# Seven-product matrix multiplication for both feed-forward products, with the squared hidden rows staged in DRAM

## The chip, the cores and the metric

The kernel runs on one core of a Trainium2 chip. TensorE (PE) multiplies matrices into PSUM, VectorE (DVE), ScalarE (ACT) and GpSimd (POOL) work on tiles in SBUF or PSUM, and SyncE (SP) issues most of the DMA transfers. The metric is the time of one execution on the device in microseconds, median of three runs.

## The reference

One step of a two-layer decoder trunk over 1024 prompt tokens and 32 sample tokens (8 sequences of 4), 1056 tokens of width 1024. Everything is fp32.

```python
for i in range(DEPTH):                       # DEPTH = 2
    hp = rms_norm(xp, norm_mix[i]); hs = rms_norm(xs, norm_mix[i])
    if i % N_MIXERS == 0:                    # layer 0: spatial-gating MLP in chunks of 128
        ...
    else:                                    # layer 1: indexer, top 256 keys per query, attention
        ...
    xp = xp + op; xs = xs + os_
    xp = xp + sqrelu_mlp(rms_norm(xp, norm_ffn[i]), ffn_w1[i], ffn_w2[i])
    xs = xs + sqrelu_mlp(rms_norm(xs, norm_ffn[i]), ffn_w1[i], ffn_w2[i])
y = rms_norm(x, norm_final)

def sqrelu_mlp(h, w1, w2):                   # w1: 1024 x 4096, w2: 4096 x 1024
    a = jax.nn.relu(h @ w1)
    return (a * a) @ w2
```

The outputs are the normalized rows, the new keys, values and indexer keys, and the chunk rows of layer 0. The sample sequences attend to 1024 cached positions each, fetched by a page table.

## The kernel before

Tokens lie along the free dimension, features along the 128 partitions. The 1056 tokens form three chunks of 384, 384 and 288 (`CH`). Each fp32 operand of a large product is split in a high and a low part: `split` (L201) writes the high part on ScalarE (L203) and the rest on VectorE (L204), or on GpSimd where `lo_w` says so; with a gain it uses L206 and L207. `mm3` (L240) makes one product of three matmuls (L242, L247, L248): high by high, high by low, low by high.

The residual lies in SBUF as `X`. `out_proj` adds the mixer's projection to it (L500), sums the squares (L299, L300) and splits the gain-scaled rows into `H`; the scale of a token, `rbc`, comes from `norm_chunk` and is applied only after the up product, so the matmuls needn't wait for it.

`ffn` runs over 32 tiles of 128 hidden rows. A tile's up product is plain: 8 products `mm3` for each chunk. VectorE applies relu and `rbc` (L526), ScalarE squares into `st` (L539). Two tiles make a block (`FB`). For 15 of the 16 blocks the down product is in the seven-product scheme: both operands are cut in 2 x 2 parts, seven products of sums of the parts replace eight. The left operand is 256 hidden rows by 256 outputs (four pairs of output tiles, `m`), the right one 256 hidden rows by 528 tokens (two halves, `pr`), so a matmul has 264 columns (`SN`). `combine0` and `combine1` make the right sums on GpSimd (L550 to L558) and split them into `A2`; `w2_block` makes the weights' sums on GpSimd (L568 to L571) and splits 1024 columns. `w2_pair` issues the matmuls (L590 to L592); each result is added into `X`: six on VectorE, `u7` copied by ScalarE (L603) and added twice by GpSimd (all L581). The up products of the next block's first tile stand between the pairs. The last block is plain, with `done` behind each output tile and chunk: `done0` writes the rows to DRAM and splits the next layer's input, `done1` prepares the final norm, and `final` transposes and writes the outputs.

In the attention, `sample_keys` transposes the cached keys of two sequences and computes their dots, `sample_mask` spreads the selection, `sample_softmax` works for one key head over all eight sequences, `fetch_values` reads the values into `H`'s memory, and `sample_values` multiplies.

The order of the instructions on each engine is set by a scheduler that simulates the program when it is built; each engine then works in that order, and tiles of a pool with few buffers are reused in turn.

## Time and profile before

| | |
|---|---|
| median of 3 runs | 2442.8 us (2439.52 to 2445.67) |
| the profiled execution | 2439.28 us, span 2436.9 us |
| TensorE busy | 2336.8 us, 96% |
| weight loads | 2246.2 us, 92% |
| VectorE busy | 1692.9 us, 69% |
| GpSimd busy | 1310.4 us, 54% |
| ScalarE busy | 1062.5 us, 44% |
| TensorE's mean granted clock | 0.982 of full speed |
| DMA | 158.38 MB, mean 65 GB/s |

The busy time of an engine is the union of its instructions. Matmuls are pipelined: one of 264 columns shows as 0.28 us though the next starts long before it ends, so their pace is read from start to start. The span leaves out some 2 us around the program.

### The profile page before, as it was taken

The page shows a single profiled execution, that of the slowest core. Times are in us where ns is not written, and L with a number is a line of the kernel's source. Part 1 is how long each engine was busy: PE and PEld are TensorE (multiplying, and loading weights), DVE is VectorE, ACT ScalarE, POOL GpSimd, SP SyncE. Part 2 cuts the span into 40 slices and gives each one's busy share as a digit, 9 for nine tenths or more (in the row PEclk, how much of TensorE's full clock was granted, in tenths as well). Part 3 has the DMA queues.
Part 4 walks back from the last instruction along what each step waited for, and adds up shares of the span by engine and source line. Part 5 has one row for each costly group of instructions (what it writes and reads, how often), then busy time and mean ns, then how long its engine had stood idle before and what let it go on. Part 6 is the DMA issues. An engine that isn't in the chain of part 4 may idle for free.

```text
span 2436.9 us, 42780 instructions
## 1 busy us (share of the span) xinstructions
PE 2336.8 (96%) x15961; PEld 2246.2 (92%) x15961; DVE 1692.9 (69%) x3732; ACT 1062.5 (44%) x2164; POOL 1310.4 (54%) x1695
## 2 busy tenths in 40 slices
PE   8999999999999999989988968999999999999998
PEld 7999999999999999988988747899999999999998
DVE  6151257777777777774998879735677777777775
ACT  6232243333333333355865767734333333333335
POOL 2245446676676676561224435414566766766754
PEclk9999999999999999999999979999999999999999
DMA  6211301111111111141223441040111111111111
GB/s 231 61 46 35 123 27 46 47 48 49 44 48 48 49 52 40 55 131 30 84 70 104 142 173 27 10 158 27 44 48 45 48 49 45 51 46 49 53 44 72
DMA packets 180800, 158.38 MB, mean 65 GB/s; under 512 B 10376, under 2 KB 169712, under 8 KB 179568
## 3 DMA queue, kind: packets, MB, share of 16 engines
...
q0 software_dynamic: 4096, 18.88, 2.3%
...
## 4 chain that ended last, share of the span: by engine, by line
PE 35%; DVE 9%; POOL 4%; issue 4%; ACT 2%; DMA 1%; SPq 0%; another core or an unknown queue 0%; DVEq 0%; POOLq 0%; ACTq 0%
PE ps L242 4%; PE ps L248 4%; PE ps L247 3%; PE px L242 3%; PE px L248 3%; PE px L247 3%; PE ps L590 2%; PE ps L591 1%; PE ps L592 1%; DVE sc L895 1%; POOL st L558 1%; PE pt L1138 1%; PE pt L592 1%; PE pt L591 1%; PE pt L590 1%
## 5 line engine op out<-in xcount | busy, mean ns | idle before, releaser
L581 POOL TENSOR_TENSOR X<-X,scr 128x264 f32<-128x264 f32 x480 | 427.0, 913 | 165.0 <-DVE X L581 119.4
L248 PE MATMUL ps<-h,w 128*128 128x384 f32 (+1 forms) x1344 | 438.3, 326 | 1.6 <-POOL w L204 1.4
L242 PE MATMUL ps<-h,w 128*128 128x384 f32 (+1 forms) x1344 | 437.1, 325 | 0.7 <-DVE scr L909 0.4
L247 PE MATMUL ps<-h,w 128*128 128x384 f32 (+1 forms) x1344 | 435.8, 324 | 0.0
L203 ACT ACTIVATE w<-raw 128x1024 fp32r<-128x1024 f32 (+2 forms) x248 | 250.6, 1012 | 305.6 <-PE px L247 123.3
L204 DVE TENSOR_TENSOR w<-raw,w 128x1024 fp32r<-128x1024 f32 (+1 forms) x211 | 298.4, 1414 | 32.9 <-ACT w L203 32.6
L242 PE MATMUL px<-h,w 128*128 128x384 f32 (+1 forms) x960 | 310.8, 324 | 0.3
L248 PE MATMUL px<-h,w 128*128 128x384 f32 (+1 forms) x960 | 309.8, 323 | 0.0
L247 PE MATMUL px<-h,w 128*128 128x384 f32 (+1 forms) x960 | 309.2, 322 | 0.0
L603 ACT ACTIVATE scr<-ps 128x264 f32<-128x264 f32 x240 | 92.7, 386 | 426.4 <-PE ps L592 380.3
L248 PEld LDWEIGHTS ps<-h,w 128*128 128x128 f32 x1344 | 254.4, 189 | 3.1 <-POOL w L204 1.7
L242 PEld LDWEIGHTS ps<-h,w 128*128 128x128 f32 x1344 | 254.6, 189 | 2.4 <-ACT w L203 1.0
L247 PEld LDWEIGHTS ps<-h,w 128*128 128x128 f32 x1344 | 254.4, 189 | 0.6
L581 DVE TENSOR_TENSOR X<-X,ps 128x264 f32<-128x264 f32 x480 | 197.4, 422 | 64.3 <-PE ps L592 64.3
L581 DVE TENSOR_TENSOR X<-X,px 128x264 f32<-128x264 f32 x480 | 194.2, 422 | 52.2 <-PE px L592 52.2
L581 DVE TENSOR_TENSOR X<-X,pt 128x264 f32<-128x264 f32 x480 | 203.1, 423 | 33.7 <-PE pt L592 29.0
L590 PE MATMUL ps<-A,w 128*128 128x264 f32 x720 | 206.8, 288 | 20.2 <-ACT A L203 20.2
L591 PE MATMUL ps<-A,w 128*128 128x264 f32 x720 | 206.6, 290 | 7.6 <-DVE A L204 7.5
L592 PE MATMUL ps<-A,w 128*128 128x264 f32 x720 | 203.6, 284 | 0.0
L568 POOL TENSOR_TENSOR raw<-raw 128x128 f32<-128x128 f32 x120 | 56.6, 472 | 267.7 <-DMA raw<-in_ffn_w 178.1
L204 DVE TENSOR_TENSOR A<-st,A 128x264 fp32r<-128x264 f32 (+2 forms) x184 | 164.1, 905 | 45.7 <-ACT A L203 45.6
L242 PEld LDWEIGHTS px<-h,w 128*128 128x128 f32 x960 | 180.4, 188 | 1.3 <-DVE X L581 1.2
...
## 6 DMA issues: line engine op xcount, KB each, us to landing
...
raw<-in_ffn_w SPq DMA_DIRECT2D x120, 256.0 KB
...
```

Of the source, the lines that this page charges most:

```text
L203: S.activation(hi, src, AF.Copy)
L204: (lo_w[0] or V).tensor_tensor(lo, src, f(hi), op=ALU.subtract)
L242: PE.matmul(out, lh, rh, start=first, stop=False)
L247: PE.matmul(out, lh, rl, start=False, stop=False)
L248: PE.matmul(out, ll, rh, start=False, stop=last)
L558: G.tensor_tensor(q[:, 1], q[:, 2], q[:, 1], op=ALU.subtract)
L568: G.tensor_tensor(sm[0], a21, a22, op=ALU.add)
L581: eng.tensor_tensor(x, x, src, op=op)
L590: PE.matmul(p, wh, xh, start=first, stop=False, skip_group_check=not first)
L591: PE.matmul(p, wh, xl, start=False, stop=False, skip_group_check=not first)
L592: PE.matmul(p, wl, xh, start=False, stop=True, skip_group_check=not first)
L603: S.activation(u, p, AF.Copy)
```

## The change

Both feed-forward products are in the seven-product scheme. `wino` issues seven products of `nk` times three matmuls of 264 columns. `out_proj` keeps three residual rows at a time, writes them to DRAM (`x_out`) and leaves gain-scaled rows in `XG`, one tile per half of 528 tokens (`TH`). `combos` makes the seven right sides of the up product for a half, each 4 x 264 columns, and splits them into slots of the pools `c8`, `ca`, `cb` and `cc`. `w1_block` makes the weights of 256 hidden rows. The products are summed into a tile `c` of four quarters, then `squares` applies relu and `rbc`, squares, makes four sums of the squares (`t`) and writes all eight tiles to DRAM, `hd`. The down product runs after the up product is complete: `hidden` reads one right side of 512 hidden rows (540 KB) and splits it, `w2_block` makes the weights, `block` adds the products into `XS` and `U`. The sum `u7` is collected in `U` and added to both its quarters in the last 512 rows. The residual is added by a GpSimd DMA that accumulates, in the third of the eight. In the last 512 rows the first two pairs of output tiles are done whole, the other two by halves of the tokens, with `done` behind each.

The sample attention handles four sequences per group: `sample_keys` does one sequence at a time beside the value tiles, `sample_softmax` both key heads of four sequences, and `fetch_values` comes ahead of it. `H` is one tile, or a list of tiles of `c8`.

```diff
-FB = 2
+NB = DF // 512
-SLOT = {(0, 0): 2, (0, 1): 3, (1, 0): 1, (1, 1): 0}
-PRODS = (("v5", 4, 1, True), ("u1", 0, 0, True), ("v3", 7, 2, False), ("u6", 5, 5, False), ("q4", 3, 4, True),
-         ("p2", 2, 3, True), ("u7", 6, 6, False))
+TH = T // 2
+PRODS = (("v5", True), ("u1", True), ("v3", False), ("u6", False), ("q4", True), ("p2", True), ("u7", False))
+HID = {"u1": 0, "p2": 2, "v3": 3, "v5": 4, "u6": 5, "u7": 6, "q4": 7}
...
+    def out_proj(w, gain, pre, x_in, x_out):
...
         def after(p, o, c, sl):
-            V.tensor_tensor(X[:, o, sl], p, X[:, o, sl], op=ALU.add)
-            sumsq(X[:, o, sl], o, c)
+            x = rows[o][:, sl]
+            V.tensor_tensor(x, p, x, op=ALU.add)
+            sumsq(x, o, sl)
+            for pr in range(2):
+                a, b = max(sl.start, pr * TH), min(sl.stop, (pr + 1) * TH)
+                if a < b:
+                    S.activation(XG[pr][:, o, a - pr * TH:b - pr * TH], rows[o][:, a:b], AF.Copy, scale=gain[:, o:o + 1])
+            if c == NC - 1:
+                SP.dma_start(x_out[o // 2][o % 2], rows[o])
...
+    def wino(nk, wt, xt, pr, post):
+        banks = {}
+        for key, first in PRODS:
+            if first:
+                banks[key[0]] = ps({"u": "ps", "v": "px"}.get(key[0], "pt"))
+            p = banks[key[0]][:, :SN]
+            kw = dict(skip_group_check=not first)
+            for k in range(nk):
+                wh, wl, xh, xl = wt(key, 0, k), wt(key, 1, k), xt(key, pr, 0, k), xt(key, pr, 1, k)
+                PE.matmul(p, wh, xh, start=first and k == 0, stop=False, **kw)
+                PE.matmul(p, wh, xl, start=False, stop=False, **kw)
+                PE.matmul(p, wl, xh, start=False, stop=k == nk - 1, **kw)
+            post(key, p)
+            yield
+    def run(*blocks):
+        for _ in PRODS:
+            for g in blocks:
+                next(g)
+    def summed(outs, add=False):
...
+        def post(key, p):
+            if key == "v5":
+                start(p, 3)
+            elif key == "u1":
+                start(p, 0)
+            elif key == "v3":
+                v3.append(p)
+            elif key == "u6":
+                start(p, 1)
+                V.tensor_tensor(outs[1], v3[0], outs[1], op=ALU.add)
+            elif key == "q4":
+                start(p, 2, ALU.subtract)
+            elif key == "p2":
+                V.tensor_tensor(outs[0], p, outs[0], op=ALU.add)
+            else:
+                V.tensor_tensor(outs[2], p, outs[2], op=ALU.add if add else ALU.subtract)
+                V.tensor_tensor(outs[3], p, outs[3], op=ALU.add)
+        return post
...
+    def w1_block(w1, fb, kk):
...
+        w_sums((s1, s2, s4, s3), a11, a21, a12, a22)
+        wt = {}
+        for key, src in (("v5", s1), ("u1", a11), ("v3", s4), ("u6", s2), ("q4", a22), ("p2", a12), ("u7", s3)):
+            wt[key] = wslot([P, 2, 4, P])
+            split(wt[key][:, 0], wt[key][:, 1], src)
+        return lambda key, z, k: wt[key][:, z, k]
+    def w2_block(w2, fb, m):
...
+        wt = {}
+        for keys, src in ((("v5", "u6"), sm[:, 0:2]), (("u1",), r[:, :, 0, 0]), (("v3", "u7"), sm[:, 2:4]),
+                          (("p2",), r[:, :, 1, 0]), (("q4",), r[:, :, 1, 1])):
+            if keys[0] != "q4":
+                t = wslot([P, 2, 2, 2, P])
+            q = 1 if keys[0] == "q4" else 0
+            if len(keys) == 2:
+                split(t[:, 0], t[:, 1], src)
+            else:
+                split(t[:, 0, q], t[:, 1, q], src)
+            for z, key in enumerate(keys):
+                wt[key] = t[:, :, z + q]
+        return lambda key, z, k: wt[key][:, z, k]
+    def ffn(layer, XG, sx, x_in, done):
...
+        def combos(pr, homes):
+            b11, b12, b21, b22 = (XG[pr][:, 4 * i:4 * i + 4, j * SN:(j + 1) * SN] for i in range(2) for j in range(2))
+            t1, t2, t3, t4 = (raw([P, 4, SN]) for _ in range(4))
+            def put(key, src, eng=None):
+                t = HC[pr][key] = homes[key]([P, 2, 4, SN])
+                lo_w[0] = eng
+                split(t[:, 0], t[:, 1], src)
+                lo_w[0] = None
+            V.tensor_tensor(t1, b12, b11, op=ALU.subtract)
+            put("v5", t1)
+            put("u1", b11)
+            V.tensor_tensor(t3, b22, b12, op=ALU.subtract)
+            put("v3", b22, G)
+            V.tensor_tensor(t2, t3, b11, op=ALU.add)
+            put("u6", t2)
+            V.tensor_tensor(t4, t2, b21, op=ALU.subtract)
+            put("q4", t4)
+            if pr:
+                S.activation(t1, b21, AF.Copy)
+                sx[1].close()
+                st, home = slots("cc", 2)
+                sx.append(st)
+                homes["p2"] = homes["u7"] = home
+                b21 = t1
+            put("p2", b21, G)
+            put("u7", t3)
+        def squares(c4, fb, kk, pr):
+            c = c4.rearrange("p (i j) t -> p i (j t)", i=2)
+            rb = rbc[:, None, pr * TH:(pr + 1) * TH].to_broadcast([P, 2, TH])
+            V.scalar_tensor_tensor(c, c, 0.0, rb, op0=ALU.max, op1=ALU.mult)
+            S.activation(c, c, AF.Square)
+            t = fh.tile([P, 4, SN], F32, name="t")
+            G.tensor_tensor(t[:, 0:4:2], c4[:, 1:4:2], c4[:, 0:2], op=ALU.subtract)
+            G.tensor_tensor(t[:, 1], t[:, 2], c4[:, 0], op=ALU.add)
+            G.tensor_tensor(t[:, 3], t[:, 1], c4[:, 2], op=ALU.subtract)
+            for z, x in ((0, c4), (4, t)):
+                SP.dma_start(hd[fb][z:z + 4, :, kk, pr].rearrange("j p t -> p j t"), x)
...
+        wt = w1_block(w1, 0, 0)
+        combos(0, dict(zip(keys, [ca] * 2 + [c8] * 5)))
+        sx[0].close()
...
+        for fb in range(NB):
+            for kk in range(2):
+                if fb or kk:
+                    wt = w1_block(w1, fb, kk)
                 for pr in range(2):
+                    c4 = fh.tile([P, 4, SN], F32, name="c", bufs=3)
+                    run(wino(4, wt, xt1, pr, summed([c4[:, q] for q in range(4)])))
+                    squares(c4, fb, kk, pr)
+                    if fb == kk == pr == 0:
+                        combos(1, dict(zip(keys, [cb] * 2 + [c8] * 3)))
...
+        XS = [fp.tile([P, 2, T], F32, name="x%d" % m) for m in range(4)]
+        U = [fp.tile([P, 2, SN], F32, name="u%d" % m) for m in range(4)]
...
+        def hidden(fb, some):
+            for key in some:
+                s = (nth[0] + 4) % 10
+                nth[0] += 1
+                t = A2[fb, key] = (c8 if s < 8 else ca)([P, 2, 2, 2, SN])
+                r = raw([P, 2, 2, SN])
+                SP.dma_start(r, hd[fb][HID[key]])
+                split(t[:, 0], t[:, 1], r)
...
+            def by_pool(x, p):
+                s = scr(SN)
+                S.activation(s, p, AF.Copy)
+                G.tensor_tensor(x, x, s, op=ALU.add)
...
+            def post(key, p):
+                if key in ("u1", "p2"):
+                    add(c11, p)
+                elif key in ("v3", "u6"):
+                    add(c12, p)
+                elif key == "q4":
+                    add(c21, p, ALU.subtract)
+                elif fb < NB - 1:
+                    by_pool(c22 if key == "v5" else u, p)
+                elif key == "v5":
+                    add(c22, p)
                 else:
+                    add(u, p)
+                    add(c21, u)
+                    add(c22, u)
+            return wino(2, wt, lambda key, pr, z, k: A2[fb, key][:, z, k, pr], pr, post if fb else post0)
+        hidden(0, keys)
+        for fb in range(NB - 1):
+            for z in range(4):
+                m = z if fb else 3 - z
+                wt = w2_block(w2, fb, m)
+                run(*(block(fb, m, pr, wt) for pr in range(2)))
+                if z < 3:
+                    hidden(fb + 1, keys[z:z + 1])
+                if fb == 2:
+                    G.dma_start(out=XS[m], in_=x_in[m].rearrange("o p t -> p o t"), accum_op=ALU.add)
+            hidden(fb + 1, keys[3:])
+        fb = NB - 1
+        for m in range(2):
+            wt = w2_block(w2, fb, m)
+            run(*(block(fb, m, pr, wt) for pr in range(2)))
+            for i in range(2):
+                done(XS, 2 * m + i, slice(0, T), c8)
+        wts = {m: w2_block(w2, fb, m) for m in (2, 3)}
+        for pr in range(2):
+            run(*(block(fb, m, pr, wts[m]) for m in (2, 3)))
+            for o in range(4, NK):
+                done(XS, o, slice(pr * TH, (pr + 1) * TH), c8)
...
+    def done0(X, o, sl, c8):
+        x = X[o // 2][:, o % 2, sl]
+        SP.dma_start(xb[o // 2][o % 2, :, sl], x)
+        sumsq(x, o, sl)
+        if sl.start == 0:
+            H.append(c8([P, 2, T]))
+        hsplit(x, o, sl, G_MIX[1])
         if o == NK - 1:
+            for c in (range(1, NC) if sl.start else range(1)):
+                norm_chunk(c)
...
     for i in range(NT):
         value_tile(i)
-        if 2 <= i < 8:
-            sample_keys(i - 2)
-    probs = []
-    for kv in range(2):
-        probs.append(scores(0, kv))
-        sample_keys(6 + kv)
-    sample_mask()
-    for kv in range(2):
-        sample_softmax(kv)
+        if i:
+            sample_keys(i - 1)
     fetch_values()
     for z in range(2):
+        sample_softmax(z)
+    probs = [scores(0, kv) for kv in range(2)]
+    for z in range(2):
         sample_values(z)
-    H = hidden_state()
+    hst.close()
+    hst, H = hidden_state("hB")
```

VectorE before, at the start of the first feed-forward block: `h` are the split rows of the last chunk, `dg` the diagonals of the norm, `w` weights of the next up tiles, `scr<-px` the relu pass of the first up product.

```order
L272 TENSOR_SCALAR rst_81<-pt_3248 128x3
L207 SCALAR_TENSOR_TENSOR h2_71<-X_2516,gains_78,h2_71 128x288 x2
L500 TENSOR_TENSOR X_2516<-ps_3294,X_2516 128x288
L207 SCALAR_TENSOR_TENSOR h2_71<-X_2516,gains_78,h2_71 128x288
L283 TENSOR_SCALAR dg_3255<-one_72,rst_81 128x128
L283 TENSOR_SCALAR dg_3258<-one_72,rst_81 128x128
L207 SCALAR_TENSOR_TENSOR h2_71<-X_2516,gains_78,h2_71 128x288 x2
L204 TENSOR_TENSOR w_3585<-raw_3578,w_3584 128x1024
L207 SCALAR_TENSOR_TENSOR h2_71<-X_2516,gains_78,h2_71 128x288
L526 SCALAR_TENSOR_TENSOR scr_3389<-px_3364,rbc_80 128x384
```

VectorE in the changed kernel at the same place: `c` are slots of right sides, `raw` their unsplit sums, `xg0` and `xg1` the gain-scaled rows of the two halves; c_3435 is the right side of the product that TensorE does first.

```order
L661 TENSOR_TENSOR raw_3568<-xg1_2535 128x1056
L221 TENSOR_TENSOR c_3446<-raw_3431,c_3446 128x1056
L221 TENSOR_TENSOR c_3450<-raw_3433,c_3450 128x1056
L221 TENSOR_TENSOR c_3456<-raw_3432,c_3456 128x1056
L664 TENSOR_TENSOR raw_3570<-xg1_2535 128x1056
L221 TENSOR_TENSOR c_3435<-raw_3430,c_3435 128x1056
L666 TENSOR_TENSOR raw_3569<-raw_3570,xg1_2535 128x1056
L221 TENSOR_TENSOR c_3438<-xg0_2539,c_3438 128x1056
L289 TENSOR_SCALAR rst_79<-pt_3365 128x2
L289 TENSOR_SCALAR rst_79<-pt_3365 32x1
L668 TENSOR_TENSOR raw_3571<-raw_3569,xg1_2535 128x1056
L221 TENSOR_TENSOR c_3584<-raw_3569,c_3584 128x1056
```

The splits of single tiles' chunks have become splits of 1056 columns, and that of the first product's right side stands fourth among them. On ScalarE its high part comes after the writes of the residual rows to DRAM, since its slot lies on their memory.

VectorE before, at the end of a block of the down product: adds into `X`, weights of 1024 columns, and splits of the next block's right sides into `A2`.

```order
L204 TENSOR_TENSOR A2_3357<-st_6466,A2_3357 128x264
L581 TENSOR_TENSOR X_2516<-X_2516,ps_6602 128x264
L581 TENSOR_TENSOR X_2516<-X_2516,pt_6638 128x264
L526 SCALAR_TENSOR_TENSOR scr_6700<-ps_6675,rbc_80 128x384
L204 TENSOR_TENSOR w_6899<-raw_6892,w_6898 128x1024
L204 TENSOR_TENSOR A2_3357<-scr_6657,A2_3357 128x264
L526 SCALAR_TENSOR_TENSOR scr_6729<-px_6704,rbc_80 128x384
L204 TENSOR_TENSOR A2_3357<-scr_6663,A2_3357 128x264
L526 SCALAR_TENSOR_TENSOR scr_6765<-ps_6740,rbc_80 128x288
L204 TENSOR_TENSOR A2_3357<-st_6355,A2_3357 128x528
L581 TENSOR_TENSOR X_2516<-X_2516,ps_6802 128x264
```

VectorE in the changed kernel between two groups of 512 hidden rows of the down product: adds into `x3`, the last pair's tile, splits of the next group's right sides (`c`), then its first weights (`w`).

```order
L221 TENSOR_TENSOR c_10203<-raw_10204,c_10203 128x1056
L737 TENSOR_TENSOR x3_7331<-x3_7331,px_10084 128x264
L737 TENSOR_TENSOR x3_7331<-x3_7331,px_10094 128x264
L221 TENSOR_TENSOR c_10208<-raw_10209,c_10208 128x1056
L737 TENSOR_TENSOR x3_7331<-x3_7331,ps_10104 128x264
L221 TENSOR_TENSOR c_10213<-raw_10214,c_10213 128x1056
L737 TENSOR_TENSOR x3_7331<-x3_7331,pt_10164 128x264
L221 TENSOR_TENSOR w_10225<-raw_10219,w_10225 128x512
L221 TENSOR_TENSOR w_10228<-raw_10218,w_10228 128x256
L737 TENSOR_TENSOR x3_7331<-x3_7331,ps_10112 128x264
L221 TENSOR_TENSOR w_10231<-raw_10219,w_10231 128x512
L737 TENSOR_TENSOR x3_7331<-x3_7331,pt_10172 128x264
```

Four splits of 1056 columns (the first stands five rows ahead of these) are now among the last pair's adds, where splits of 264 to 792 columns stood, and the next group's weights come behind them.

## Rows read from the trace of the kernel before

**Rows 1.** Busy time in four stretches (us: stretch, length, engines, TensorE's clock, DMA share, GB/s).

```profile
338.70:1067.30 728.60, 712.50 (x4993) 704.66 (x4991) 556.52 (x1090) 276.38 (x571) 470.40 (x610) 1.00 0.17 52
1693.90:2424.20 730.30, 715.96 (x5029) 709.09 (x5027) 545.93 (x1080) 277.71 (x575) 470.49 (x615) 1.00 0.15 46
1067.30:1100.00 32.70, 26.23 (x174) 23.73 (x174) 18.65 (x41) 9.09 (x21) 22.96 (x47) 0.85 0.33 101
2424.20:2437.00 12.80, 5.94 (x55) 5.54 (x53) 4.98 (x9) 5.75 (x12) 3.55 (x5) 0.92 0.69 264
```

**Rows 2.** Timeline of TensorE: first and last matmul of three runs (start us, us, instruction).

```profile
221.33 0.34 PE L242 MATMUL ps<-h,w 128*128 128x384 f32 x1
...
237.91 0.34 PE L248 MATMUL ps<-h,w 128*128 128x384 f32 x1
238.09 0.29 PE L242 MATMUL ps<-h,w 128*128 128x288 f32 x1
...
244.35 0.29 PE L248 MATMUL ps<-h,w 128*128 128x288 f32 x1
...
2378.11 0.29 PE L590 MATMUL ps<-A,w 128*128 128x264 f32 x1
...
2383.09 0.28 PE L592 MATMUL pt<-A,w 128*128 128x264 f32 x1
```

**Rows 3.** TensorE's waits, 338.7 to 1067.3 (us in total, times, longest us).

```profile
PE ps L590 <- ACT A L203: 10.2, 14, 0.8
PE ps L591 <- DVE A L204: 4.2, 13, 0.7
```

**Rows 4.** VectorE by line and form (count; busy us, mean ns; idle before, releasers).

```profile
L204 DVE TENSOR_TENSOR w<-raw,w 128x1024 fp32r<-128x1024 f32 x203 | 290.5, 1431 | 32.9 <-ACT w L203 32.6 <-issue 0.3
L581 DVE TENSOR_TENSOR X<-X,pt 128x264 f32<-128x264 f32 x480 | 203.1, 423 | 33.7 <-PE pt L592 29.0
...
L204 DVE TENSOR_TENSOR A<-st,A 128x528 fp32r<-128x528 f32 x64 | 54.2, 847 | 16.3 <-ACT A L203 16.2
...
L204 DVE TENSOR_TENSOR A<-st,A 128x264 fp32r<-128x264 f32 x60 | 37.7, 628 | 1.6 <-ACT A L203 1.6
L207 DVE SCALAR_TENSOR_TENSOR h<-X,gains,h 128x384 fp32r<-128x384 f32 x48 | 37.5, 804 | 3.8 <-ACT h L206 3.7
L526 DVE SCALAR_TENSOR_TENSOR scr<-ps,rbc 128x384 f32<-128x384 f32 x64 | 35.4, 554 | 118.6 <-PE ps L248 71.4 <-ACT w L203 38.2 <-ACT scr L603 4.7
```

**Rows 5.** ScalarE by line and form.

```profile
L203 ACT ACTIVATE w<-raw 128x1024 fp32r<-128x1024 f32 x220 | 233.1, 1060 | 290.0 <-PE px L247 123.3 <-PE ps L591 72.2 <-POOL raw L571 37.5
L603 ACT ACTIVATE scr<-ps 128x264 f32<-128x264 f32 x240 | 92.7, 386 | 426.4 <-PE ps L592 380.3 <-POOL X L581 46.1
...
L203 ACT ACTIVATE A<-st 128x528 fp32r<-128x528 f32 x64 | 40.9, 640 | 1.0
```

**Rows 6.** Waits of the DMA queue's engine.

```profile
SPq L921 <- DMA qd<-scr: 16.1, 6, 5.2
```

**Rows 7.** Timeline of TensorE at the end of the first feed-forward block.

```profile
1067.13 0.30 PE L248 MATMUL ps<-A,w 128*128 128x288 f32 x1
...
1070.13 0.42 PE L242 MATMUL ps<-w,h 128*32 128x292 f32 x1 [2.15 <-ACT h L206]
1070.35 0.45 PE L247 MATMUL ps<-w,h 128*32 128x292 f32 x1
1070.60 0.45 PE L248 MATMUL ps<-w,h 128*32 128x292 f32 x1
```

**Rows 8.** GpSimd by line and form.

```profile
L581 POOL TENSOR_TENSOR X<-X,scr 128x264 f32<-128x264 f32 x480 | 427.0, 913 | 165.0 <-DVE X L581 119.4 <-ACT scr L603 30.8 <-DVE w L204 12.8
...
L204 POOL TENSOR_TENSOR w<-raw,w 128x512 fp32r<-128x512 f32 x20 | 26.2, 1320 | 77.5 <-ACT w L203 69.5 <-DVE idh L470 7.8
```

**Rows 9.** Timeline of ScalarE in the attention stretch.

```profile
1422.19 0.63 ACT L203 ACTIVATE t<-raw 128x512 fp32r<-128x512 f32 x1 [10.19 <-issue]
```

**Rows 10.** Timeline of VectorE in the same stretch.

```profile
1423.30 0.16 DVE L967 RECIPROCAL rc<-sd 128x1 f32<-128x1 f32 x1 [7.58 <-ACT w L966]
```

425 lines of the change are left out of this document (191 added, 234 removed).

## The prediction

> **What bounds the kernel now.** I read the summary by engine first: TensorE is busy for 96% of the span, VectorE 69%, GpSimd 54%, ScalarE 44%. Then the busy time by stretches: the two feed-forward blocks, from their first up matmul to their last down matmul, last 728.60 and 730.30 us [rows 1], 60% of the span, and TensorE works for 98% of that at its full clock (1.00, the 2.4 GHz level). So I price this change in matmuls first and in waits of TensorE second. The timeline of TensorE gives the pace, start to start: 96 matmuls of 384 columns from 221.33 to 237.91 us, (237.91 − 221.33)/95 = 0.1745 us; 48 of 288 columns, (244.35 − 238.09)/47 = 0.1332; 42 of 264 columns, (2383.09 − 2378.11)/41 = 0.1215 [rows 2]. Last I read TensorE's waits in the first block: the largest two are for the split of the hidden rows, 14 times and 13 times, at most 0.8 us each [rows 3].
>
> By these paces one feed-forward block is 1536 × 0.1745 + 768 × 0.1332 (up product) + 2520 × 0.1215 (15 down blocks) + 96 × 0.1745 + 48 × 0.1332 (the last, plain block) = 268.0 + 102.3 + 306.2 + 16.8 + 6.4 = 699.7 us. The stretches are 28.9 and 30.6 us longer: 59.5 us is lost today, in many gaps of under a microsecond.
>
> **What the matmuls give.** After: up 8 × 2 × 2 × 7 × 4 × 3 = 2688 matmuls, down 8 × 4 × 2 × 7 × 2 × 3 = 2688, all of 264 columns: 5376 × 0.1215 = 653.2 us. That is 46.5 us less per block, **−93.0** for both. This part is firm; the rest is how much more TensorE waits.
>
> **Start of each block.** The first product's right side is now a combination made of the gain-scaled rows. The order shows that its split comes after three other splits, and its slots lie where the residual rows were, so it also waits until these are written to DRAM. From the last matmul of the projection: the add (0.55 us at 384 columns, like the eviction in rows 4), the write of the rows, the high part on ScalarE (1.06, rows 5), before the first matmul. The nearest row of a wait for a DRAM write is 16.1 us in 6 times, mean 2.7, longest 5.2 [rows 6]; I take 3.5 for half a megabyte. The Trainium skill (DMA: Bandwidth & Descriptors, Anatomy of one DMA) gives about 2.0 us fixed plus bytes over 436 GB/s for a transfer; for 540 KB that makes an estimate of 3.2 us, inside this row's span, so the sum by it would be 0.3 us lower at each place. Gap: 0.55 + 3.5 + 1.06 = 5 us. After a gap TensorE comes back at half its clock: at 1070.13, after 2.15 us idle, 292-column matmuls start 0.24 us apart instead of 0.13 [rows 7]; over the 32.7 us around it the mean clock is 0.85, at most 0.15 × 32.7 = 4.9 us lost [rows 1]. I take 3. Price 8 us per block; 0 if the splits run ahead under the projection, 15 if the landing takes the longest row twice.
>
> **Steady up product.** A weight unit is 168 matmuls = 20.4 us of TensorE. VectorE has 7 splits of 128x512 (0.85, by the 128x528 row), 8 adds (0.42) and two passes over 1056 (1.431 × 1056/1024 = 1.475): 6.0 + 3.4 + 3.0 = 12.4 us [rows 4]. GpSimd: 4 sums of 512 (1.32, the row of its 128x512 split) and two sets of three, 2 × (1.35 + 2 × 0.913): 11.6 us [rows 8]. ScalarE: 8 copies at 0.386, 2 squares at 1.1, 7 high parts at about 0.6: 9.5 [rows 5]. All have room; I leave 5 us per block for stray waits.
>
> **Between the products.** Four sum tiles of the down product lie on memory that the square tiles hold until their last write to DRAM has left. From the last up matmul: two adds 0.84, the relu pass 1.475, the square 1.1, GpSimd's three sums 3.2, the write 3.5, the copy into the tile 0.39: 10.5 us. TensorE meanwhile has 8 groups of 6 matmuls, 48 × 0.1215 = 5.8 us, before all its banks are full. Stall 4.7, half clock 3: **8 us** per block (2 to 16).
>
> **Steady down product.** Per 512 hidden rows TensorE has 4 output pairs × 2 halves × 7 × 2 × 3 = 336 matmuls, × 0.1215 = 40.8 us. VectorE: 40 adds × 0.422 = 16.9; weights 4 × (2 × 0.85 + 3 × 0.628) = 14.3; 7 splits of 1056, 7 × 1.475 = 10.3; together 41.5 us [rows 4]. So VectorE becomes the second bound, level with TensorE, and in its row it is not evenly loaded: three pairs have 4.2 + 3.6 + 1.5 = 9.3 us beside 10.2 us of TensorE, but the fourth has four of the splits, 4.2 + 3.6 + 5.9 = 13.7, ahead of the next block's weights. TensorE waits there for 3.5 us, since the banks of the adds queued behind come free late: 6 boundaries × 3.5 = **21 us** per block. Floor 0 (the adds and splits here are means under GpSimd's competition, and slack of the other pairs may absorb the surge), ceiling 46 (VectorE never gets beyond 85% busy: 41.5/0.85 = 48.8, 8 us more per boundary, less the first).
>
> **Last 512 rows.** VectorE takes all sums itself: 72 × 0.422 = 30.4, weights 14.3: 4 us over TensorE's 40.8. In the first block eight splits of the next layer's input come on top: 1056 columns at 0.804/384 per column, 2.2 us, 17.7 in all, of which the last four half-columns fall behind the end anyway. I take +14 and +6 (4 to 22 for the pair's dearer one).
>
> Losses then: first block 8 + 5 + 8 + 21 + 14 = 56, second 8 + 5 + 8 + 21 + 6 = 48; together 104 against today's 59.5: **+44.5**.
>
> **The ends.** The last step now closes 528 tokens at once instead of 288. The end after the last matmul takes 12.80 us now, at 264 GB/s [rows 1]; three more tiles of 0.52 MB at that rate are 6.0 us, with their evictions **+7** (2 to 12). The first block's end, for the same reason, +2.
>
> **Sample attention.** Groups of four sequences put the keys' work beside the value tiles and the value fetch ahead of the softmax. Today ScalarE sits 10.19 us and VectorE 7.58 us idle near 1412 to 1423 us [rows 9, 10]; that may go, at most −12 with what follows it. Against it, value reads of 8 MB now run beside the softmax and delay the prompt's probabilities: +12. I take **0**.
>
> Sum against the profiled execution, 2439.28 us (span 2436.9 and 2.4 around it): −93.0 + 44.5 + 7 + 2 = −39.5, 2399.8. The median of the runs shown is 3.5 above the profiled one, so 2403.
>
> **Rivals.**
> *The waits are hidden.* VectorE's means fall when GpSimd stops adding 480 times into X (rows 8 shows 427 us of it), a boundary costs 1 us and a start 3: losses 3 + 5 + 8 + 6 + 14 = 36 and 28, net −93 + 64 − 59.5 + 9 = −79.5: 2363 (2340 to 2380). For it: today VectorE, at 76% in the block, makes TensorE wait little. Against: the splits now stand four in a row.
> *Dearer joints.* Starts and joints at their upper ends (15 and 16), attention +6: +7 × 2 + 8 × 2 + 6 = 36 above the forecast: 2439, within a few us of no change.
> *VectorE decides: slower.* In the down product VectorE, at 41.5 us of work against 40.8, runs in order with adds that wait for matmuls and splits that wait for ScalarE and for DRAM reads; at 85% a block is 48.8 us, 4.5 more than forecast, × 12 = 54: 2457. It decides from 39.5/12 = 3.3 us above my price, some 47.6 us per 512 rows. For it: nowhere in these stretches is VectorE above 76%. Against: adds released early pair well with long splits.
> *Square tiles hold up the up product: slower.* One buffer takes the sums of squares; its next use waits for its write to land. Each half has 10.2 us; sums 3.2 + write 5.2 + queueing behind half-megabyte weight reads on the same queue could exceed it. At 2 us for each of 64 halves: +128, 2531. Against: 3.2 + 3.5 = 6.7 fits.
> *A matmul has a fixed price, so more matmuls are slower.* The counts go from 4968 to 5376 per block. By rows 2 the price per column is (0.1745 − 0.1215)/120 = 0.44 ns and only 5 ns are fixed, which denies it; if it were all fixed, 699.7/4968 = 0.1408 each, a block's matmuls would take 57 us more, and the kernel 2443 + 115 + 53.5 = 2611. The Trainium skill (TensorE: Matmul & The Clock Gate, Back-to-back issue gap) gives sustained 81 ns at 128 columns and 131 at 512; by that, an estimate of 99, 102 and 114 ns at our widths, a block's matmuls would take 12 us more and the kernel 2443 + 24 + 53.5 = 2520. The trace has 0.1215 us where this says 0.099 and 0.1745 where it says 0.114: the rows decide.
>
> **How the numbers follow.** Forecast 0.45, its own range 2380 to 2430 (floors and ceilings of boundary and joints half used); hidden waits 0.23; dearer joints 0.12; VectorE decides 0.13; square tiles 0.05; fixed price 0.02. About 0.3% (7 us) can be told from no change. Faster: 0.45 + 0.23 and a little of the third, 0.70. The same: most of the third, 0.10. Slower: the last three, 0.20. Range 2355 to 2460: it leaves out the low half of the hidden waits (0.10) and the last two rivals with a tail (0.10).
>
> **What would show it.** Matmuls at 264 columns 0.1215 us apart throughout; blocks of 653 us plus 48 to 56; a gap of 5 us with the half clock at each block's start and between its products; TensorE's longest waits in the down product at the blocks' first pairs, released by VectorE; VectorE above 85% there. The prediction is wrong if the up product waits for GpSimd or DRAM writes in every unit, if blocks of the down product take under 42 us or over 47, or if the attention stretch moves by more than 12 us.

## The result: slower, and the profile after

The changed kernel takes 2497.51 us (median of 4 runs, 2495.17 to 2501.59) against 2442.3 for the kernel before: ratio 1.0234, 95% interval 1.0221 to 1.0247. The forecast was 2403, with a range up to 2460. The span of the profiled execution grew from 2436.9 to 2499.5 us. Its page, first the engines, then TensorE's share and granted clock in 40 slices:

```profile
PE 2299.6 (92%) x16817; PEld 2198.9 (88%) x16817; DVE 1685.8 (67%) x3214; ACT 1204.2 (48%) x2385; POOL 1275.8 (51%) x1287
...
PE   8999879999979899989988989997999997989997
...
PEclk9999989999989999989999979998999998999998
```

TensorE has less to do and waits more; the clock falls at new places. By matmul starts the 62.6 us come from: the first projection ends 10.4 us later (338.94 before, 349.34 now); its gap to the first product grew from 0.13 to 9.7 us, in both layers (+19.1); the two feed-forward blocks, first to last matmul, take 745.8 and 740.0 us instead of 728.1 and 729.6 (+28.1); the stretch between them is 1.0 longer, the end 3.9.

The first block in stretches that follow its work (columns as in [rows 1]): first weight unit, the other fifteen but the last's end, change from up to down product with the first group of 512 hidden rows, groups two to seven, last group.

```profile
359.04:389.90 30.86, 25.31 (x179) 24.80 (x180) 26.92 (x29) 16.90 (x26) 18.65 (x9) 0.80 0.27 82
389.90:697.50 307.60, 306.13 (x2511) 305.91 (x2509) 203.51 (x257) 134.89 (x253) 180.66 (x147) 1.00 0.51 167
697.50:759.50 62.00, 47.61 (x348) 47.19 (x349) 29.20 (x49) 31.75 (x71) 24.59 (x25) 0.86 0.38 123
759.50:805.30 45.80, 42.47 (x338) 41.34 (x336) 38.30 (x67) 21.34 (x45) 29.42 (x30) 1.00 0.43 137
805.30:859.30 54.00, 45.43 (x338) 44.05 (x337) 43.93 (x70) 21.65 (x47) 35.53 (x37) 0.94 0.70 173
859.30:908.30 49.00, 43.53 (x338) 42.75 (x337) 38.81 (x66) 19.65 (x41) 28.99 (x33) 0.97 0.50 141
908.30:955.60 47.30, 43.86 (x339) 42.79 (x337) 38.72 (x71) 21.68 (x47) 31.93 (x32) 0.96 0.41 128
955.60:1002.80 47.20, 42.23 (x336) 41.37 (x337) 39.10 (x69) 20.54 (x44) 33.22 (x34) 1.00 0.41 126
1002.80:1046.00 43.20, 41.77 (x339) 41.13 (x337) 38.32 (x63) 19.15 (x41) 30.77 (x31) 1.00 0.41 125
1046.00:1104.90 58.90, 52.76 (x390) 49.85 (x390) 54.79 (x111) 29.51 (x56) 32.99 (x32) 0.94 0.35 119
```

A weight unit at the pace of [rows 2] is 20.4 us, a group 40.8. The up product's steady part runs at that pace (units of 20.5 us) although VectorE, ScalarE and GpSimd all work there. Nearly everything is lost at joints, where one stage hands over to the next, and in the last group. TensorE's waits from the end of the projection to the end of the block, against the many short ones of [rows 3]:

```profile
PE px L560 <- ACT w L220: 20.0, 14, 3.8
PE px L560 <- ACT x L746: 10.8, 1, 10.8
PE pt L301 <- DVE dg L300: 6.4, 2, 4.7
PE px L561 <- DVE c L221: 5.5, 1, 5.5
```

The largest sum is for the high part of the first weights of a group (L220), not for VectorE's adds. A wait costs more than itself: behind a longer one matmuls start 0.22 us apart instead of 0.1215, which is the lower level of the clock, 1.2 GHz, and the mean granted clock of those stretches is 0.94 to 0.97. In groups two to seven that holds for 61 matmuls of the first block and 80 of the second, 6 and 8 us.

GpSimd's, ScalarE's and TensorE's timelines at the boundary before 908 us show why the weights come late; their load was issued at 892.25 and had landed at 895.8.

```profile
897.75 0.75 POOL L742 TENSOR_TENSOR u<-u,scr 128x264 f32<-128x264 f32 x1 [5.81 <-ACT scr L741]
899.09 1.47 POOL L742 TENSOR_TENSOR u<-u,scr 128x264 f32<-128x264 f32 x1 [0.58 <-ACT scr L741]
900.52 1.48 POOL L742 TENSOR_TENSOR x<-x,scr 128x264 f32<-128x264 f32 x2
901.95 0.74 POOL L602 TENSOR_TENSOR raw<-raw 128x256 f32<-128x256 f32 x1
902.65 1.76 POOL L605 TENSOR_TENSOR raw<-raw 128x256 f32<-128x256 f32 x1
```

```profile
906.14 0.94 ACT L220 ACTIVATE w<-raw 128x512 fp32r<-128x512 f32 x2 [2.21 <-POOL raw L603]
```

```profile
906.82 0.39 PE L560 MATMUL px<-c,w 128*128 128x264 f32 x1 [1.36 <-ACT w L220]
```

GpSimd stands idle for 5.8 us with the weights' sums queued behind additions that wait for ScalarE's copy of a product not yet done. Only then come the sums, the second of them 1.76 us long beside VectorE's splits where the first took 0.74, then ScalarE's high part and the matmul.

### The profile page after: what moved, and what is told of

Same layout as the page of the kernel before. It is cut to its first block, busy times and chain, and to the rows that moved or that the text cites. A ratio compares the mean times of both kernels' runs of the same rounds, so it can differ in the third digit from the quotient of the medians.

```text
span 2499.5 us, 44052 instructions
## 1 busy us (share of the span) xinstructions
PE 2299.6 (92%) x16817; PEld 2198.9 (88%) x16817; DVE 1685.8 (67%) x3214; ACT 1204.2 (48%) x2385; POOL 1275.8 (51%) x1287
## 5 line engine op out<-in xcount | busy, mean ns | idle before, releaser
L221 DVE TENSOR_TENSOR w<-raw,w 128x512 fp32r<-128x512 f32 (+3 forms) x567 | 473.9, 856 | 153.9 <-ACT w L220 145.8
L220 ACT ACTIVATE w<-raw 128x512 fp32r<-128x512 f32 (+3 forms) x604 | 334.6, 582 | 321.0 <-POOL raw L603 155.5
L560 PE MATMUL ps<-c,w 128*128 128x264 f32 x1536 | 442.8, 290 | 11.2 <-DVE x L737 8.2
L561 PE MATMUL ps<-c,w 128*128 128x264 f32 x1536 | 441.0, 288 | 0.0
L562 PE MATMUL ps<-c,w 128*128 128x264 f32 x1536 | 435.3, 287 | 0.0
L560 PE MATMUL px<-c,w 128*128 128x264 f32 x1024 | 298.5, 292 | 59.2 <-ACT w L220 35.3
L560 PE MATMUL pt<-c,w 128*128 128x264 f32 x1024 | 297.9, 291 | 11.5 <-DVE x L737 9.7
L560 PEld LDWEIGHTS ps<-c,w 128*128 128x128 f32 x1536 | 294.7, 192 | 15.2 <-DVE x L737 10.0
L561 PE MATMUL px<-c,w 128*128 128x264 f32 x1024 | 295.4, 289 | 11.1 <-DVE c L221 11.1
L562 PE MATMUL pt<-c,w 128*128 128x264 f32 x1024 | 293.3, 289 | 7.1 <-DVE w L221 7.1
L562 PE MATMUL px<-c,w 128*128 128x264 f32 x1024 | 293.3, 290 | 3.1 <-DVE w L221 3.1
L561 PE MATMUL pt<-c,w 128*128 128x264 f32 x1024 | 295.7, 289 | 0.0
L561 PEld LDWEIGHTS ps<-c,w 128*128 128x128 f32 x1536 | 294.6, 192 | 0.0
L562 PEld LDWEIGHTS ps<-c,w 128*128 128x128 f32 x1536 | 292.0, 192 | 0.0
L560 PEld LDWEIGHTS px<-c,w 128*128 128x128 f32 x1024 | 197.3, 193 | 66.0 <-ACT w L220 40.9
L221 DVE TENSOR_TENSOR c<-raw,c 128x1056 fp32r<-128x1056 f32 x128 | 202.2, 1587 | 36.7 <-ACT c L220 36.1
L560 PEld LDWEIGHTS pt<-c,w 128*128 128x128 f32 x1024 | 196.9, 192 | 14.0 <-DVE x L737 11.4
L561 PEld LDWEIGHTS px<-c,w 128*128 128x128 f32 x1024 | 197.2, 193 | 11.7 <-DVE c L221 11.7
L562 PEld LDWEIGHTS pt<-c,w 128*128 128x128 f32 x1024 | 195.9, 192 | 8.2 <-DVE w L221 8.2
L562 PEld LDWEIGHTS px<-c,w 128*128 128x128 f32 x1024 | 196.7, 194 | 3.9 <-DVE w L221 3.7
L561 PEld LDWEIGHTS pt<-c,w 128*128 128x128 f32 x1024 | 197.2, 193 | 0.0
L602 POOL TENSOR_TENSOR raw<-raw 128x256 f32<-128x256 f32 (+1 forms) x96 | 123.0, 1281 | 144.1 <-DVE c L221 64.0
## 6 DMA issues: line engine op xcount, KB each, us to landing
x<-xa POOLq DMA_DIRECT2D x4, 1056.0 KB, 10.3
```

Of the source, the lines that this page charges most:

```text
L220: S.activation(hi, src, AF.Copy)
L221: (lo_w[0] or V).tensor_tensor(lo, src, f(hi), op=ALU.subtract)
L560: PE.matmul(p, wh, xh, start=first and k == 0, stop=False, **kw)
L561: PE.matmul(p, wh, xl, start=False, stop=False, **kw)
L562: PE.matmul(p, wl, xh, start=False, stop=k == nk - 1, **kw)
L602: G.tensor_tensor(s1, a21, a22, op=ALU.add)
```

## The experiments

All times are medians of 4 to 10 runs beside runs of the kernel before on the same chip (2439 to 2441 us there, 2442.3 beside the changed kernel), so a difference of 4 us or less between two runs tells nothing. Each edit also makes the order of every engine anew, so places far from the edit move too. Group times are from the first matmul to the next group's first.

**e1: without the residual's transfers.**

```diff
-                if fb == 2:
-                    G.dma_start(out=XS[m], in_=x_in[m]..., accum_op=ALU.add)
```

> Leaves out the addition of the residual rows in the third group of the down product (four GpSimd DMAs of 1 MB with accumulation). In the changed kernel's trace this group takes 54.0 and 53.7 us where its neighbours take 45.8 and 49.0 (45.6 and 46.9). Theory A (the accumulating DMA holds GpSimd's queue and the sum tile while it runs): the group falls to about 46 us in both blocks, -16 in all, and the gaps of 4.1 and 3.4 us near 826 and 854 us go; 2497 becomes about 2480. Rival (the group is long because of the weights' chain, as at the other boundaries): it stays above 51 us, the kernel within 5 us.

2479.91 us, ratio 1.0169 (1.0152 to 1.0186). The third group falls from 54.0 to 46.0 (second block 53.7 to 45.8): theory A. Others move as well, the fifth from 47.3 to 43.7 in both blocks and the first block's first and last groups up by 1.7 and 1.6. In the changed kernel the transfer waits at the head of GpSimd's order for VectorE, and takes 10.3 us to land (the page's DMA issues). The additions and sums that it held back then run in one row on GpSimd, and beside them a VectorE split that takes 1.25 us elsewhere takes 6.87; the add that TensorE waits for stands behind this split.

```profile
822.08 1.37 POOL L783 DMA_DIRECT2D x<-xa  x1 [2.90 <-DVE x L737]
```

```profile
822.62 6.87 DVE L221 TENSOR_TENSOR c<-raw,c 128x1056 fp32r<-128x1056 f32 x1
```

```profile
829.89 0.59 PE L560 MATMUL pt<-c,w 128*128 128x264 f32 x1 [3.81 <-DVE x L737]
```

**e2, e3: less work in the down product, for VectorE or for GpSimd. e4: the same work, weights earlier.**

```diff
# e2, in hidden()
-                split(t[:, 0], t[:, 1], r)
+                S.activation(t[:, 0], r, AF.Copy)    # block() then reads the high part in both places
# e3, in w2_block(); the loaded parts r are split in place of the sums
-        w_sums([sm[:, z] for z in range(4)], ...)
# e4, in ffn()
-                wt = w2_block(w2, fb, m)
+                wt = weights(fb, m)      # also makes those of the next pair, in program order ahead of this pair's matmuls
```

> In the down product the low part of the hidden rows is not computed (the high part is used in its place), so VectorE loses seven instructions of 1056 columns, about 10 us, of its 41 us per 512 hidden rows; matmuls stay. Theory of the prediction (VectorE's throughput sets the waits at the group boundaries): groups two and four to seven, now 43.2 to 49.0 us, fall to 41 to 42, in all -50 to -60 us with the other groups: about 2440. Rival (the next group's first weights come late, because their sums stand in GpSimd's order behind adds that wait for the last matmuls): the waits for the first weights stay, -10 to -20: about 2482.

> In the down product the four sums of the weights on GpSimd are left out (the loaded parts are split in their place), 128 instructions per block, and with them one of the two buffers each weight load takes. Rival theory (weights' chain through GpSimd): the waits of TensorE for ScalarE's weights, 20 and 13 us in the two blocks, go, and with them their followers: groups at 41 to 43 us, -40 to -60: about 2445. Theory of the prediction (VectorE's throughput): VectorE's work stays, groups at 45 to 47 us; a little faster because VectorE has less competition: -5 to -15: about 2487.

> The weights of an output pair are loaded, summed and split one pair earlier in the program; nothing else changes. Theory weights' chain: the waits for the first weights at the boundaries go, -30 to -50: about 2455. Theory VectorE's throughput: the work is the same, within 8 us of 2497. A third possibility: the earlier loads take the buffers that the hidden rows need, and the waits move to those: 2497 or above.

e2: 2427.85 us (0.9947, 0.9931 to 0.9964); groups two to seven 40.9, 44.0, 43.8, 41.8, 41.8, 41.4. e3: 2439.26 (0.9997, 0.9988 to 1.0007); 41.1, 46.0, 43.5, 43.1, 43.2, 43.2. e4: 2480.29 (1.0162, 1.0145 to 1.0179); 41.8, 47.3, 48.9, 44.7, 44.7, 43.3. e2 and e3 each did what its own theory said, or more, so alone they decide nothing: with less on VectorE the weights' low parts and GpSimd's sums beside them are done sooner as well (in e2's first block no wait for the first weights is listed in groups two to seven), and without the sums VectorE has less competition. e4 changes no work. Its 17 us lie between its two theories. TensorE's longest waits in groups two to seven, first block, of the changed kernel, and of e4 that for the first weights:

```profile
PE px L560 <- ACT w L220: 16.1, 13, 3.2
PE pt L560 <- DVE x L737: 4.7, 2, 3.8
PE ps L560 <- DVE x L737: 3.4, 3, 2.1
```

```profile
PE px L560 <- ACT w L220: 2.2, 2, 1.4
```

Over the floor of 6 × 40.8 us the six groups lose 41.6 us in the changed kernel and 25.8 in e4, in the second block 39.0 and 29.2: 16 and 10 us were order and latency, not work. e2 leaves 8.9 and 11.0, e3 15.3 and 16.4; less work takes away more than an earlier load does. e4's kernel gained only 17 in all: the first block's last group became 61.8 us instead of 58.9, and the stretches outside the two blocks are 5.5 longer.

**e5, e9: the start.**

```diff
# e5
-        combos(0, dict(zip(keys, [ca] * 2 + [c8] * 5)))
+        combos(0, dict(zip(keys, [c8] * 5 + [ca] * 2)))
# e9: e5, and
-            put("v3", b22, G)
+            put("v3", b22)
-            put("p2", b21, G)
+            put("p2", b21)
```

> For the first half of the tokens the first five right sides go to the slots on the old input's memory and the last two to the slots on the rows' memory, so that the one TensorE needs first no longer waits for the writes of the rows. Theory of the prediction (that wait is the gap): the first matmul of a block starts near 351 us instead of 359.0, -6 to -9 per block, 2497 becomes about 2482. Rival (the old input's memory is free only after the last matmul of the projection, and then all seven splits stand in one row on ScalarE and VectorE, whose low parts are as late as before, 365 us): the first matmul is earlier, the first unit of 31.0 us longer by as much, within 4 us of 2497.

> As e5 (first right sides in the slots that come free first), and the low parts of v3 and p2 are made by VectorE, none by GpSimd. In e5 one of those on GpSimd took 10.96 us beside VectorE's run of splits, and the sums that stand behind it came 4.8 us late. Theory (competition of the two engines, and GpSimd's order, kept what the earlier first matmul gave): first unit from 34.7 to 24-28 us, -14 to -22 against 2497 in all: about 2480. Rival (VectorE has too much there anyway: 14 splits and 8 sums of 1.25 us): 2494 or more.

e5: 2497.46 us (1.0241), no change. The first matmul comes at 351.54 instead of 359.04, as the prediction's theory has it, and the first unit takes 34.7 instead of 31.0 us, half of what the rival said. In the profiled runs the first block ends 8.2 us earlier and the second is 6.8 longer. In the changed kernel, ScalarE, VectorE and GpSimd at the start:

```profile
350.08 1.07 ACT L220 ACTIVATE c<-xg 128x1056 fp32r<-128x1056 f32 x1
351.05 2.04 ACT L220 ACTIVATE c<-raw 128x1056 fp32r<-128x1056 f32 x2
353.00 1.07 ACT L220 ACTIVATE c<-xg 128x1056 fp32r<-128x1056 f32 x1
353.97 1.07 ACT L220 ACTIVATE c<-raw 128x1056 fp32r<-128x1056 f32 x1
...
357.53 0.49 ACT L302 ACTIVATE rbc<-pt 128x384 f32<-128x384 f32 x1 [1.73 <-PE pt L301]
357.91 1.08 ACT L220 ACTIVATE c<-raw 128x1056 fp32r<-128x1056 f32 x1
```

```profile
351.63 2.57 DVE L221 TENSOR_TENSOR w<-raw,w 128x512 fp32r<-128x512 f32 x1
354.12 2.52 DVE L300 TENSOR_SCALAR dg<-one,rst 128x128 f32<-128x128 f32 x1
356.56 1.86 DVE L661 TENSOR_TENSOR raw<-xg 128x1056 f32<-128x1056 f32 x1
```

```profile
354.14 2.42 POOL L221 TENSOR_TENSOR c<-xg,c 128x1056 fp32r<-128x1056 f32 x1 [0.49 <-ACT c L220]
```

No split can begin before the projection's last matmul at 349.34, since most slots lie on its input; the one needed first is ScalarE's sixth, and its low part follows at 365.23. The sixth did not wait for the rows' write to the end: by its semaphore the last one, issued at 351.74, had landed at 354.36. What stands ahead of it at 357.53 is the copy of the token scales (`rbc`), which waited for TensorE's product with the norm's diagonals (`dg`), and these for a VectorE instruction that took 2.52 us beside GpSimd's low part. e5 moves the first split to other memory and to the head of ScalarE's order at once, so it does not tell the two apart. In e5 GpSimd's low part of `v3` became the delay, beside VectorE's row of splits, and the sum behind it held TensorE:

```profile
351.89 10.96 POOL L221 TENSOR_TENSOR c<-xg,c 128x1056 fp32r<-128x1056 f32 x1 [2.33 <-ACT c L220]
```

```profile
363.65 1.21 PE L285 MATMUL pt<-ones,ssum 128*128 128x1 f32 x6 [4.82 <-POOL ssum L320]
```

e9: 2489.24 (1.0202, 1.0185 to 1.0219), 8 us, half of what was expected; first units 33.5 and 32.2 us. So GpSimd's low parts were part of it. The longest wait left in the first unit, 3.6 us, is for GpSimd's sum of squares, which takes 8.16 us beside VectorE's row of splits (1.25 for the one before it); 47 matmuls at half the pace cost another 4.6.

```profile
353.39 8.16 POOL L320 TENSOR_TENSOR ssum<-ssum,scr 128x288 f32<-128x288 f32 x1 [4.70 <-ACT scr L318]
```

**e6: the first projection.**

```diff
-    raw_bufs(3)                  # ahead of layer 0
+    raw_bufs(5)
...
-    raw_bufs(5)                  # ahead of its projection
```

> The five load buffers exist from the kernel's start; before, they were three there and were made anew ahead of the first projection, on memory in use. Theory (the projection's weights could not be loaded until that memory was free, near 256 us, which is the 10.7 us by which it ends later than before the change): weights arrive early, the gap of 4.5 us at 259 us goes, -4 to -8: about 2491. Rival (the rows' loads, on the memory of the mixer's input, are what it waits for): within 2 us of 2497.

2489.6 us (1.0206, 1.0189 to 1.0223). No wait of TensorE is listed between 200 us and the end of the projection; in the changed kernel there are these:

```profile
PE ps L259 <- ACT w L220: 4.2, 1, 4.2
PE px L264 <- POOL H L221: 2.5, 1, 2.5
PE ps L264 <- POOL H L221: 1.8, 1, 1.8
```

The block starts at 347.6 us instead of 359.0. SyncE issued no load between the mixer's and 256.04 us, because the new buffers and the rows' tiles lay on memory that the mixer still used; with the weights loaded early the two waits for GpSimd's split go as well. The kernel keeps 8 us of it: the first block ends 18.2 us earlier in the profiled run, and from there to the end it is 7.1 longer.

**e7, e12, e13: between the products.**

```diff
# e7: the last half is not squared; the half before is written twice
-                    squares(c4, fb, kk, pr)
+                    if not (fb == NB - 1 and kk and pr): squares(c4, fb, kk, pr)
...   # in squares(), for the half before: the same dma_start once more, into the last half's place
# e13; with e10 and e11 below: e12
-            G.tensor_tensor(t[...], ...)
+            E = V if fb == NB - 1 and kk else G
+            E.tensor_tensor(t[...], ...)
```

> The very last half of the up product is summed but not squared or written; in its place the half before is written to DRAM twice. Theory (TensorE's wait of 10.8 and 9.9 us for ScalarE's first copy into a sum tile is the chain relu, square, sums, write of the last half): the wait falls below 3 us, the first group of the down product from 56.8 to 44-47 us, -16 to -24 in all: about 2477. Rival (the splits of the first hidden rows or the first weights are late anyway): within 6 us of 2497.

> The changed kernel with only the last 256 hidden rows' sums of squares moved from GpSimd to VectorE. Theory (one place: GpSimd's order between the products): 3 to 4 us per block, 2497 becomes about 2490. Rival (it shifts the order of the whole down product, as e12 against e11 seems to): -15 to -30.

e7: 2485.79 us (1.0189), 12 us; the first group 51.7 instead of 56.8. TensorE's wait fell from 10.8 to 5.9, not below 3. e13: 2493.51 (1.0219, 1.02 to 1.0239), 4 us, which these intervals don't tell from the changed kernel's; the wait is 8.9 us. In the changed kernel the chain runs over four engines and a write; VectorE's relu, ScalarE's square, GpSimd's first sum, the last write's issue, ScalarE's copy, TensorE (one line of each engine's timeline):

```profile
707.77 1.25 DVE L684 SCALAR_TENSOR_TENSOR c<-c,rbc 128x1056 f32<-128x1056 f32 x1
```

```profile
709.05 1.09 ACT L685 ACTIVATE c<-c 128x1056 f32<-128x1056 f32 x1 [1.37 <-DVE c L684]
```

```profile
712.66 0.72 POOL L602 TENSOR_TENSOR raw<-raw 128x256 f32<-128x256 f32 x1 [5.09 <-DMA raw<-in_ffn_w]
713.34 0.72 POOL L605 TENSOR_TENSOR raw<-raw 128x256 f32<-128x256 f32 x1
714.02 0.72 POOL L603 TENSOR_TENSOR raw<-raw 128x256 f32<-128x256 f32 x1
714.70 1.30 POOL L687 TENSOR_TENSOR t<-c 128x528 f32<-128x528 f32 x1
```

```profile
718.68 0.36 SPq L691 DMA_DIRECT2D hd<-t  x1
```

```profile
722.03 0.67 ACT L746 ACTIVATE x<-px 128x264 f32<-128x264 f32 x2 [3.88 <-DMA hd<-t]
```

```profile
722.47 0.59 PE L560 MATMUL px<-c,w 128*128 128x264 f32 x1 [10.83 <-ACT x L746]
```

The last products were read at 704.1. Two weight splits on VectorE stand ahead of the relu pass, and three weights' sums that wait for a load stand ahead of GpSimd's first sum. Even for the half before, in e7, the copy that waits for the last write starts only at 717.3.

TensorE had waited before this chain began, since its order has the down product's first matmuls ahead of the up product's last ones, and their weights hang on GpSimd's sums, which waited 10.58 us for the load:

```profile
699.86 0.59 PE L560 MATMUL px<-c,w 128*128 128x264 f32 x1 [3.84 <-ACT w L220]
```

In e4, e7 and e13 this wait stands (4.1 to 4.3 us).

**e8: the last group.**

```diff
-                    add(c22, p)
+                    by_pool(c22, p)
...
-                    add(c21, u)
-                    add(c22, u)
+                    G.tensor_tensor(c21, c21, u, op=ALU.add)
+                    G.tensor_tensor(c22, c22, u, op=ALU.add)
```

> In the last 512 hidden rows 24 of VectorE's 72 additions per block (v5 into one quarter, the collected sum into two) go to GpSimd, as v5 does in the groups before. Theory (VectorE is busy all the time from 1060 to 1090 us, so its additions set the last group): last group 58.9 and 57.4 us fall by 4 to 10 each, about 2485. Rival (GpSimd's additions, 0.74 us against 0.42, and the next layer's sums of squares behind them end later): 0 to +8.

2510.85 us (1.03, 1.0283 to 1.0317): 13 slower, the last groups 64.8 and 61.5 us. GpSimd's additions took about 1 us each (954 to 1090 ns) beside VectorE's 0.42, and it was busy 55.08 of those 64.80 us. VectorE being full does not mean that GpSimd is free.

**e10 to e12, e14 to e16: the edits together.** e10 is e4, e6 and e9; e11 issues each residual transfer one pair later; e12 adds e13's edit. e14 is e12 without e4's, e15 without the residual, e16 without the low parts and the weights' sums (as e2 and e3).

> e4 (weights a pair ahead), e6 (five buffers from the start) and e9 together. If their causes are separate places they add: -17 - 8 and what e9 gives (-14 to -22): 2450 to 2458. If they share one cause, less: above 2465.

> As e10, and each accumulating transfer of the residual is issued a pair later, when the last additions into its tile are long done. Theory (GpSimd waits with the transfer at its queue's head for those additions, 2.9 to 5.1 us each time, and the next weights' sums stand behind it): the third group falls to 44-47 us, -8 to -16 against e10. Rival (the transfer itself, 10.3 us of two half-rate streams on the same memory, is the price): within 4 us of e10.

> As e11, and the sums of the squares of the last 256 hidden rows are made by VectorE, not by GpSimd, where they stand between the sums of the first weights. Theory (GpSimd's order is 6 us of the chain behind TensorE's wait of 10.8 us): that wait falls to 4-7 us, -6 to -12 against e11. Rival (the write to DRAM, 3.3 to 5.4 us, and VectorE's own order, which is full there): within 4 us of e11.

> e12 without the loads of the weights a pair ahead. Theory (the weights' chain is a cause of its own at the boundaries): groups two to seven go from 41.6-47.2 back to 44-49, +12 to +20 against e12: about 2447. Rival (VectorE's throughput): within 5 us of e12.

> e12 without the addition of the residual. Theory (in e12 the transfer lies beside other work in the third group, but the fourth group's first pair, 16.5 us, still waits for the last of the four): the fourth group falls from 47.2 to 43-44, -6 to -9 in all. Rival (the 16.5 us are the boundary's): within 3 us.

> e12 with the low parts of the hidden rows and the weights' sums of the down product left out: VectorE has 31 us and GpSimd 15 us per 512 hidden rows beside TensorE's 40.8. If VectorE's and GpSimd's work is the loss in groups two to seven, they fall to 40.8-41.5, save for the residual's: -25 to -40 against e12, about 2395 to 2405, and the rest stays: starts 10 and 9 us, the wait between the products, the last group. If latencies hold them, less than -15.

| run | us | ratio (95%) | groups two to seven, first block |
|---|---|---|---|
| e10 | 2456.11 | 1.0064 (1.0041 to 1.0088) | 41.9 47.9 48.1 44.6 44.4 43.3 |
| e11 | 2455.20 | 1.0066 (1.0049 to 1.0083) | 42.1 47.3 50.0 45.3 44.5 43.5 |
| e12 | 2430.62 | 0.9967 (0.9957 to 0.9977) | 41.6 43.6 47.2 44.6 43.8 44.4 |
| e14 | 2482.36 | 1.0170 (1.0135 to 1.0206) | 45.8 53.9 45.0 45.7 46.9 43.2 |
| e15 | 2432.18 | 0.9967 (0.9957 to 0.9978) | 41.7 42.8 44.2 44.5 44.4 43.3 |
| e16 | 2385.78 | 0.9776 (0.9758 to 0.9794) | 41.0 41.4 45.6 41.0 41.0 40.9 |

In e10 the three parts add up and more (−41.4 against −33.4 one by one), as separate causes do. e11 moved nothing: with the weights ahead the third group is already at 47.9 and stays at 47.3, and the fourth takes 50.0. e12 is faster than both kernels, 0.33% below the one before. Its own place gave 3 to 4 us per block (the wait is 9.5 us, in e11 13.3); the rest of the 25 came in groups and in the last group (61.3 to 55.6, 56.6 to 52.3), where the order of all engines is another. e14 shows what carries it: without the weights ahead e12 is 52 us slower, three times what was expected and more than e4's 17 suggest; its groups are nearly those of the changed kernel, in the second block the same to 0.3 us but for the fourth. e15 against e12 is no difference: its third and fourth groups gain 4, its last group is 61.5. e16, 45 us under e12, takes the six groups to 250.9 us, 6 over the floor (4 in the second block), against 20 in e12; so 14 and 16 us go with VectorE's and GpSimd's work. It leaves out links of the weights' chain too, so it does not tell busy engines from a long chain. What e16 still loses: first unit 31.1 us, wait between the products 8.1, last group 54.7.

## Why the prediction was wrong

By its own steps, in us, first and second block:

| step | forecast | measured |
|---|---|---|
| matmuls at 0.1215 us | 653.2 each | as forecast: steady units 20.5 |
| projection ahead of block one | not priced | 10.4 |
| start, gap and first unit | 8, 8 | 20.2, 19.8 |
| steady up product | 5, 5 | 1.2, 1.0 |
| between the products | 8, 8 | 21.2, 20.2 |
| groups two to seven | 21, 21 | 41.6, 38.9 |
| last group | 14, 6 | 18.1, 16.6 |
| ends, attention | 9 | 4.9 |

Above the forecast for the profiled run, 2399.8 against 2501.6, stand in both blocks together: groups two to seven 38.5 us, the change of products 25.4, the starts 24.0, the last groups 14.7, and the projection 10.4; the steady up product took 7.8 less.

- **The saving was right**, and the rule of the Trainium skill that the prediction weighed (TensorE: Matmul & The Clock Gate, Back-to-back issue gap) is again not what the trace shows: by it the estimate was 0.099 us, and matmuls of 264 columns start 0.122 us apart in the median here, as [rows 2] have it.
- **Steady down product: the failing step, mechanism half right.** The prediction put a boundary at VectorE's surge alone, 3.5 us each, 21 per block, and nothing for the weights' chain through GpSimd's order, for the residual's transfer or for the half clock behind a wait; 41.6 and 38.9 us were lost. It said that VectorE would release the longest waits there: 16.1 us wait for the high part of the weights, 8.1 (4.7 and 3.4) for VectorE's adds. Weights a pair ahead take 16 and 10 us away with the same work (e4; e14 the other way round). Without the residual the six groups lose 15 and 13 us less (e1). The two overlap: either brings the third group from 54 to 46 or 47, and in e12 the transfer costs the kernel nothing (e15). With the weights ahead and the transfer a pair later e12 still loses 20 in each block, and 14 and 16 of that go with VectorE's and GpSimd's work (e16). The surge was thus near its size, but how much of it is VectorE's alone isn't shown.
- **Between the products: one wait priced, a chain there.** It added the right steps, 10.5 us, but each as if its engine were free; in the trace they take from 704.1 to 722.0, 18 us, since VectorE and GpSimd had weights ahead of them. Another 4 us were lost ahead of it in the wait at 699.86, and 2.5 in the second block. The write itself was as priced: 3.35 us from issue to the copy. The Trainium skill (DMA: Bandwidth & Descriptors, Anatomy of one DMA) gave an estimate of 3.2, by a fit that it makes for GpSimd's queue, while this write is SyncE's. e7's last write, beside loads, took 7.9.
- **Start: the wrong wait.** The rows' last write had landed 5.0 us after the projection's last matmul, 4.05 were priced. The high part began 3.6 us later, behind `rbc` in ScalarE's order, and behind it was the row of 14 splits that can begin only when the projection's input is free: TensorE waited 5.5 us more for the first low part. An earlier first matmul alone (e5) gave nothing. The half clock was sized about right here: 20 matmuls of the first unit 0.22 us apart, 2.0 us against the 3 priced.
- **Last group.** 18.1 us against 14, and 16.6 against 6 in the second block, where VectorE was busy for 45.7 of 57.7 us. No run isolates this.
- **The rival "Dearer joints"**, 2439, had two of the right places, and still less than they cost: 15 and 16 us against 20.2 and 21.2 in the first block.
- **The rival "VectorE decides"**, 2457, had the sign but not the cause: VectorE's busy share in groups two to seven is 79 to 89%, and the same work runs 16 and 10 us per block faster in another order. That VectorE's work is a part is plain from e2.
- **Square tiles** and the steady up product were no problem, as forecast. The attention's 0 was two guesses of 12 us against each other; the stretch between the blocks is 1.0 longer, and no run tells why, so that it came out may be luck.

What stays open: why e12's order gains more than its parts. The order of every engine is made anew from the whole program, and a run tells only what it became. A rival to GpSimd's order also stands untested: the five load buffers. In groups two to seven of the first block SyncE's loads of hidden rows waited 120.8 us, 24 times, for VectorE (put down to its adds, L737), and no run has more buffers; e3 and e16 need one less for each load of weights, along with what else they leave out.
